# First feed-forward: the first two gate blocks from the scaled residual, with norm and shift joined in behind the products

## The chip, the cores and the metric

The kernel runs on one core of one Trainium2 chip. The metric is the device time of one execution in microseconds (us). Five engines work side by side, each through its own instructions in order: TensorE (PE, with its weight loads shown as PEld), VectorE (DVE), ScalarE (ACT), GpSimd (POOL) and the queue of transfers (SP).

## The reference

Two blocks of two layers each stand behind each other. The change touches the seam in layer 0 of the first block, between the state-space mixer and the feed-forward network. With x of 256 tokens by 1024 channels:

```
g   = gelu(y)
x   = x + gate1 * (g * sigmoid(g @ w_glu + b_glu))
h   = rms_norm(x, norm2_g) * (1 + scale2) + shift2
ff  = (silu(h @ w_gate) * (h @ w_up)) @ w_down
x   = x + gate2 * ff
```

`rms_norm` divides each token by the root of its mean square (plus 1e-6) and multiplies each channel by its gain. The feed-forward width is 2816, which is 22 blocks of 128 columns.

## The kernel before, in words

Everything is held with channels on the partitions: x is a tile of 128 x 8 x 256, eight blocks `k` of 128 channels by 256 tokens. Products are made in three parts, because weights and activations are each split into a rounded high part and the remainder: high by high, high by low, low by high (`mm3`). One such part is one matmul of 128 x 128 weights by 256 tokens. The weights come as tiles of 1 MB (`raw`, sixteen blocks of 128 x 128) through a ring of six buffers, in the order of one transfer queue (SP). Each tile is split in four quarters of 128 x 512: ACT makes the high part (`whi`), DVE the low part (`wlo`), and the four buffers of each are used in turn, so that a split waits until PE has finished the quarter four places back.

A scheduler orders each engine's instructions from the order in which the code was written; stretches under `manual_schedule` keep the written order on PE.

The stretch concerned:
- `proj(glu, ...)` multiplies by w_glu, two column blocks at a time (tiles `ps_mm`). `evac` then makes for each block `ob` the sigmoid (`sg`, ACT), its product with gelu (`sg`, DVE) and the new residual (`x`, DVE), and hands the square (`sq`, ACT) to `sumsq`. POOL adds the first six squares; the sum over channels is made by products with a matrix of ones into `ps_aux`.
- `root()` closes the sum, scales it (`rstd`, DVE) and takes the power -1/2 (`rstd`, POOL).
- `spread` copies it out along the free axis (`sprd`, ACT) and transposes it, so that every partition holds the factor of each token (L330).
- `ffn(0)` splits the first tile of gate weights ahead (`early`), then `normed` makes for each k the scaled x (`nrm`, DVE), adds the shift and rounds (`hh`, ACT) and makes the remainder (`hl`, DVE).
- For each p of 11, the products of two gate blocks (`pg`) and two up blocks (`pu`) follow, 48 matmuls each. For p = 0 and gate they go channel block by channel block, as `hh` and `hl` come. Then come silu (ACT), the product with `pu` (DVE) and its split (`ah`, `al`).
- After each of the 22 groups of 48 matmuls `pump` lets one step of a waiting matrix-vector product run (the modulations of the next layer): for the first six groups these are four operations `acc` of 128 x 512 on DVE each, from one tile `kvada`.

Of the kernel before, what the change touches and what calls it, by code (L numbers as in the profile page):

```python
# [9 lines left out]
F32 = mybir.dt.float32  # L10
F32R = mybir.dt.float32r
I32 = mybir.dt.int32
AF = mybir.ActivationFunctionType
ALU = mybir.AluOpType
AX = mybir.AxisListType

D, T, FF = 1024, 256, 2816
# [204 lines left out]
class _Flow:  # L222
# [12 lines left out]
    def add(self, rank, steps):  # L235
        self.strands.append([rank, self.t, (), steps])
        self.strands.sort(key=lambda s: s[0])
# [44 lines left out]
def _go(steps, n=1 << 30):  # L282

    for _ in range(n):
        if next(steps, steps) is steps:
            break


class K:
# [100 lines left out]
    def stream(self, src):  # L390

        raw, cur = {}, {}

        def get(n, ahead=False):
            t, u = n // 16, n // 4
            if u not in cur:
                if t not in raw:
                    raw.clear()
                    raw[t] = self.wtile(src[t])
                cur[u] = self.wsplit(raw[t], (u % 4) * WS, WS)  # L400
            if ahead:
                return
            for o in [o for o in cur if o < u]:
                del cur[o]
            hi, lo = cur[u]
            s = slice((n % 4) * 128, (n % 4 + 1) * 128)
            return hi[:, s], lo[:, s]

        return get
# [235 lines left out]
    def s5(self):  # L645
        nc, tc, a, c = self.nc, self.tc, self.a, self.c
        cp = self.cp
        V, G, S_ = nc.vector, nc.gpsimd, nc.scalar
        with ExitStack() as ctx:
            pool = lambda name, bufs=1: ctx.enter_context(tc.tile_pool(name=name, bufs=bufs))  # L650
            sm, big = pool("s5sm"), pool("s5big")
# [3 lines left out]
            B8 = lambda tag, shape, name, n=1, dt=F32: (old if tag in ("bc", "D", "P") else big).tile(  # L655
                shape, dt, tag=tag, name=name, bufs=n)
# [13 lines left out]
            box = []  # L670
# [15 lines left out]
            t = lambda n, w=32: sm.tile([128, w], F32, name="d_" + n)  # L686
# [25 lines left out]
            rs = sm.tile([128, 8], F32, name="rs")  # L712
# [91 lines left out]
            for e in range(8):  # L804
# [18 lines left out]
                for q in range(4):  # L823
                    o = psK[32 * q:32 * q + 32, 0:128]
# [18 lines left out]
            U = B8("U", [128, 16, 128], "U")  # L843
# [3 lines left out]
            for h in range(2):  # L847
                f = slice(8 * h, 8 * h + 8)
# [3 lines left out]
                for j4 in range(2):  # L852
# [4 lines left out]
                    o = U[:, 8 * h + 4 * j4:8 * h + 4 * j4 + 4].rearrange("p j n -> p (j n)")  # L857
# [38 lines left out]
            for k in range(1, 8):  # L896
                n = 4 if k < 7 else 3
                a8 = lambda k: A8[:, k].unsqueeze(1).to_broadcast([128, n, 2, 32])
                u2 = sm.tile([128, 4, 2, 32], F32, tag="u2", name="u2", bufs=2)
                f = slice(k, k + 8 * n - 7, 8)  # L900
# [4 lines left out]
            for b in range(1, 4):  # L905
# [6 lines left out]
                for e, q in ((0, QP[:, 0:1, 0:7].to_broadcast([128, 2, 7, 32])), (1, QP[:, 1:3, 0:7])):  # L912
                    o = (St[:, 8 * b, ::-1] if e else St[:, 8 * b]).unsqueeze(1).to_broadcast([128, 7, 2, 32])
                    self.mul(w1[:, e], o, q.rearrange("p r k g -> p k r g"))
                if b < 3:
                    o = St[:, 8 * b + 8]
                    self.add(o, o, v[:, 0])
                    self.add(o, o, v[:, 1])
                o = St[:, 8 * b + 1:8 * b + 8]
# [60 lines left out]
            x1 = x0  # L980

            add, root = self.sumsq()

            def evac(ob, ps):
                sg = self.np.tile([128, T], F32, tag="sg", name="sg")
                self.act(sg, ps, AF.Sigmoid, bias=self.col("bglu", ob))
                self.mul(sg, sg, gT[:, ob].rearrange("p t c -> p (t c)"))
                self.stt(x1[:, ob].rearrange("p (c t) -> p c t", t=8), sg.rearrange("p (t c) -> p c t", t=8),
                         self.mods[0][:, 16 + ob:17 + ob], x0[:, ob].rearrange("p (c t) -> p c t", t=8), ALU.mult, ALU.add)
                add(ob, x1[:, ob])  # L990

            self.proj(glu, 0, 8, list(range(8)), lambda k: gh[:, k], lambda k: gl[:, k], evac, 24, True, True)
            self.xr = root()
            self.x = x1

# [85 lines left out]
    def ffn(self, l):  # L1083
        nc, tc, x, m = self.nc, self.tc, self.x, self.mods[l]
        self.lo = [nc.vector]
        with ExitStack() as ctx:
            self.parts(ctx, 1)
            pool = ctx.enter_context(tc.tile_pool(name=f"ffn{l}", bufs=1))
            if l:
                self.deepen(3)  # L1090
                self.fill.append(self.last(pool))
            g = self.gain(m[:, 32:40], self.col("n2", 8 * l, 8), f"g2_{l}")
            gu = self.stream(self.a[f"gu{l}"])
            with self.early(gu):
                hi, lo = self.normed(x, self.spread(self.xr, 1), g, m[:, 24:32])
            self.after = self.lowed
            ah = pool.tile([128, 22, T], F32R, name="ah")
            al = pool.tile([128, 22, T], F32R, name="al")
            for p in range(11):
                if p == 4 and l == 0:  # L1100
                    self.mla_tables()
                if p == 6:
                    self.mem_norm(l)
                pg, pu = self.ps(), self.ps()
                for i, ps in enumerate((pg, pu)):
                    if p or i:
                        for e in range(2):
                            for k in range(8):
                                wh, wl = gu(32 * p + 16 * i + 8 * e + k)
                                self.mm3(ps[:, e * T:(e + 1) * T], wh, wl, hi[:, k], lo[:, k], k == 0, k == 7)  # L1110
                    else:

                        w = [gu(n) for n in range(16)]
                        for k in range(8):
                            for e in range(2):
                                self.mm3(ps[:, e * T:(e + 1) * T], *w[8 * e + k], hi[:, k], lo[:, k], k + e == 0, k + e == 8)
                    self.pump()
                self.after = None
                t = pool.tile([128, 2 * T], F32, tag="ff", name="ff", bufs=2)
                self.act(t, pg, AF.Silu)  # L1120
                self.mul(t, t, pu)
                f = lambda z: z[:, 2 * p:2 * p + 2].rearrange("p a t -> p (a t)")
                self.split(f(ah), f(al), t)

            if l == 0:
                self.table(AF.Sqrt)
            else:
                self.drain()
            add, root = self.sumsq()

            def evac(ob, ps):
                self.stt(x[:, ob], ps, m[:, 40 + ob:41 + ob], x[:, ob], ALU.mult, ALU.add)
                add(ob, x[:, ob])

            def down():
                self.proj(self.stream(self.a[f"dn{l}"]), 0, 22, list(range(8)), lambda k: ah[:, k], lambda k: al[:, k], evac, 12, single=True)
                self.drain()


            rest = iter(itertools.chain(self.mem_keys(l), self.mem_values(l)))  # L1140
            down()
            with tc.manual_schedule(engines={mybir.EngineType.PE}):
                self.lo = [nc.vector, nc.gpsimd]
                _go(rest, 2)
                r = root()
                _go(rest, 2)
                rs = self.spread(r, 1)
                _go(rest)
            self.lo = [nc.vector]
            if l:  # L1150
                self.wparts, self.npart = self.base, 0
                self.win = self.stream(self.a["win"])
                for n in range(3):
                    self.win(4 * n, True)
                self.h = self.normed(x, rs, self.col("pre", 0, 8))
            else:
                self.xn = self.memp.tile([128, 8, T], F32, name="xr")
                for k in range(8):
                    self.mul(self.xn[:, k], x[:, k], rs)
            self.shallow()  # L1160
            if not l:
                self.accc.close()
# [1092 lines left out]
```

## Time and profile before

| | |
|---|---|
| median of 3 runs | 1089.24 us (1083.6, 1089.24, 1095.2) |
| the profiled execution | 1079.3 us, span 1077.5 us |
| PE busy | 985.0 us, 91% |
| DVE busy | 809.5 us, 75% |
| ACT busy | 580.3 us, 54% |
| POOL busy | 268.9 us, 25% |
| chain that ended last | PE 65%, DVE 15%, issue 4%, ACT 3% |

Times in the trace are counted from the start of the span. The profiled execution is 9.9 us faster than the median of the three runs. Busy shares are means over many stages; what a stage waits for is read from its own rows. "PEclk" is the granted TensorE clock as a share of 2.4 GHz, so 0.50 is 1.2 GHz.

### The profile page before, as it was taken

The numbers are of one execution on the slowest core, as the hardware profiler recorded it, in microseconds if no ns is written. First come the engines' busy times: TensorE is split into PE (matmuls) and PEld (weight loads), VectorE is DVE, ScalarE is ACT, GpSimd is POOL, SyncE is SP. The second block draws the span as 40 slices with busy tenths as digits, with TensorE's granted clock in tenths as the row PEclk, the third lists the DMA queues.
The fourth block names the chain that finished last, engine by engine and source line by source line (L and its number), as shares of the span: only waits on it lengthen the run. The fifth ranks groups of instructions, "written<-read, shape, count | busy, mean of one in ns | idle before, by whom it ended". The sixth has DMA issues, their size and how long they took to land.

```text
span 1077.5 us, 21985 instructions
## 1 busy us (share of the span) xinstructions
PE 985.0 (91%) x8490; PEld 876.3 (81%) x8490; DVE 809.5 (75%) x1771; ACT 580.3 (54%) x1301; POOL 268.9 (25%) x300
## 2 busy tenths in 40 slices
PE   3988979999999988989999999988898899799996
PEld 1446968989999866889999999987887786699984
DVE  8846788989985788779756555688887735686995
ACT  6344555556544767646555544565444344575663
POOL 7960200030011551100000001453315132243430
PEclk9999989999999989999999999999999999999999
DMA  7999439877983241255755554241312142265321
GB/s 280 375 343 372 172 142 396 307 285 294 363 329 153 98 162 73 79 196 203 267 192 174 184 195 152 104 148 54 123 40 83 36 154 99 87 232 180 134 79 40
DMA packets 29416, 198.82 MB, mean 185 GB/s; under 512 B 3744, under 2 KB 3872, under 8 KB 6528
## 3 DMA queue, kind: packets, MB, share of 16 engines
q1 hardware_dynamic: 27936, 191.73, 48.2%
q10 hardware_dynamic: 720, 3.15, 0.8%
q0 software_dynamic: 656, 2.53, 0.7%
q8 instruction: 67, 1.10, 0.4%
q14 instruction: 37, 0.30, 0.1%
HBM read 195.30 MB, written 2.10 MB: 183 GB/s over the span
## 4 chain that ended last, share of the span: by engine, by line
PE 65%; DVE 15%; issue 4%; ACT 3%; POOL 2%; DMA 1%; POOLq 0%; DVEq 0%; ACTq 0%
PE ps_mm L327 50%; PE ps_aux L327 6%; DVE wlo L306 3%; PE ps_sv L327 3%; PE ps_el L327 2%; PE ps_aux L330 2%; PE ps_st L327 2%; ACT whi L376 1%; POOL sq L306 1%; DVE Upr L306 1%; DVE acc L323 1%; DMA raw<-in_gu 1%; DVE D L1738 1%; DVE shf L319 1%; DVE A L306 0%
## 5 line engine op out<-in xcount | busy, mean ns | idle before, releaser
L376 ACT CAST whi<-raw 128x512 fp32r<-128x512 f32 (+2 forms) x488 | 296.1, 613 | 271.5 <-PE ps_mm L327 230.0
L306 DVE TENSOR_TENSOR wlo<-raw,whi 128x512 fp32r<-128x512 f32 (+2 forms) x412 | 289.1, 714 | 128.4 <-ACT whi L376 127.7
L327 PE MATMUL ps_mm<-hh,whi 128*128 128x256 f32 x1064 | 306.8, 290 | 3.0 <-ACT hh L298 2.3
L327 PE MATMUL ps_mm<-hh,wlo 128*128 128x256 f32 x1064 | 300.6, 285 | 3.4 <-DVE wlo L306 3.3
L327 PE MATMUL ps_mm<-hl,whi 128*128 128x256 f32 x1064 | 300.0, 283 | 0.2
L327 PEld LDWEIGHTS ps_mm<-hh,whi 128*128 128x128 f32 x1064 | 202.0, 190 | 8.2 <-ACT hh L298 2.9
L327 PEld LDWEIGHTS ps_mm<-hh,wlo 128*128 128x128 f32 x1064 | 200.9, 190 | 8.8 <-DVE wlo L306 7.8
L327 PEld LDWEIGHTS ps_mm<-hl,whi 128*128 128x128 f32 x1064 | 201.9, 190 | 1.3 <-DVE hl L323 0.6
L306 POOL TENSOR_TENSOR wlo<-raw,whi 128x512 fp32r<-128x512 f32 (+2 forms) x76 | 100.3, 1321 | 244.1 <-ACT whi L376 218.5
L306 POOL TENSOR_TENSOR sq<-sq 128x256 f32<-128x256 f32 x20 | 23.4, 1171 | 415.0 <-ACT sq L298 264.7
L327 PE MATMUL ps_mm<-ah,whi 128*128 128x256 f32 x352 | 99.1, 282 | 0.0
L327 PE MATMUL ps_mm<-ah,wlo 128*128 128x256 f32 x352 | 99.0, 282 | 0.1
L327 PE MATMUL ps_mm<-al,whi 128*128 128x256 f32 x352 | 98.8, 281 | 0.0
L323 DVE SCALAR_TENSOR_TENSOR acc<-raw,cs,acc 128x512 f32<-128x512 f32 x112 | 80.0, 757 | 2.2 <-DMA raw<-in_kvada 2.1
L327 PEld LDWEIGHTS ps_mm<-ah,wlo 128*128 128x128 f32 x352 | 66.3, 189 | 2.8 <-issue 1.7
L327 PEld LDWEIGHTS ps_mm<-ah,whi 128*128 128x128 f32 x352 | 67.3, 191 | 0.9 <-ACT whi L376 0.8
L327 PEld LDWEIGHTS ps_mm<-al,whi 128*128 128x128 f32 x352 | 66.4, 189 | 0.0
L327 PE MATMUL ps_gv<-raw,crep 128*32 128x512 f32 x192 | 27.3, 624 | 17.0 <-DMA raw<-in_adaH 13.7
L327 PEld LDWEIGHTS ps_gv<-raw,crep 128*32 128x32 f32 x192 | 4.5, 110 | 22.0 <-DVE pwt L306 13.7
L327 PE MATMUL ps_mm<-gl,whi 128*128 128x256 f32 x64 | 18.9, 297 | 2.4 <-DVE gl L306 2.4
L327 PE MATMUL ps_mm<-whi,ch 128*128 128x512 f32 x48 | 19.5, 437 | 1.2 <-ACT ch L422 1.2
L306 POOL TENSOR_TENSOR CE<-CE,cem 128x512 f32<-128x512 f32 x16 | 20.5, 1321 | 0.0
(552 smaller groups left out, 2037.3 us busy)
## 6 DMA issues: line engine op xcount, KB each, us to landing
raw<-in_gu SPq DMA_DIRECT2D x44, 1024.0 KB, 5.1
raw<-in_ada SPq DMA_DIRECT2D x32, 1024.0 KB, 7.2
raw<-in_dn SPq DMA_DIRECT2D x22, 1024.0 KB, 5.0
raw<-in_win SPq DMA_DIRECT2D x15, 1024.0 KB, 4.9
raw<-in_adaH SPq DMA_DIRECT2D x8, 1024.0 KB, 6.4
raw<-in_kvada SPq DMA_DIRECT2D x8, 1024.0 KB, 6.5
raw<-in_ada1h SPq DMA_DIRECT2D x8, 1024.0 KB, 5.7
raw<-in_wout SPq DMA_DIRECT2D x8, 1024.0 KB, 4.9
```

What stands on the lines that cost most here:

```text
L306: return (eng or self.nc.vector).tensor_tensor(out=out, in0=a, in1=b, op=op)
L319: (eng or self.nc.vector).tensor_scalar(out=out, in0=a, scalar1=s1, scalar2=s2, op0=op0, **kw)
L323: return self.nc.vector.scalar_tensor_tensor(out=out, in0=a, scalar=s, in1=b, op0=op0, op1=op1, **kw)
L327: return self.nc.tensor.matmul(out, l, r, start=start, stop=stop, **kw)
L330: return self.nc.tensor.transpose(out, in_, self.ident)
L376: i = self.nc.scalar.copy(out=hi[:, :width], in_=raw[:, o:o + width])
L1738: V.tensor_reduce(out=D_[64 * h:64 * h + 64, 4 * i:4 * i + 4], in_=dm[:, :, h].rearrange("p c b i -> p c i b"), axis=AX.X, op=ALU.add)
```

## The change

The products of the first two gate blocks are taken from the residual times (gain times 1 + scale), `xgh` and `xgl`, which needs neither the token factor nor the shift. The token factor is multiplied in behind the products (`ff0`, DVE). The shift times the gate weights, one number per output column, is made by sixteen products with one moving column from the unsplit weight tile (`pb`, tile `ps_gv`) and enters as the bias of silu. The two up blocks and all later ones take `hh` and `hl` as before. The splits of the first gate tile now use the mixer's four pairs of buffers, and the order of the new products on PE is written out by hand.

```
@@ def stream
-        def get(n, ahead=False):
+        def get(n, ahead=False, keep=False):
...
-                    raw[t] = self.wtile(src[t])
+                    raw[t] = self.lastraw = self.wtile(src[t])
...
-            for o in [o for o in cur if o < u]:
+            for o in [o for o in cur if o < u and not keep]:
@@ def s5 (evac, and behind it)
                 add(ob, x1[:, ob])
+                if ob < 6:
+                    return
+                if ob == 6:
+                    box[:] = [self.gain(self.mods[0][:, 32:40], self.col("n2", 0, 8), "g2_0"),
+                              B8("C", [128, 8, T], "xgh", 4, F32R), B8("U", [128, 8, T], "xgl", 1, F32R)]
+
+                g, xh, xl = box
+                for k in range(7) if ob == 6 else (7,):
+                    self.act(xh[:, k], x1[:, k], AF.Identity, scale=g[:, k:k + 1])
+                    self.stt(xl[:, k], x1[:, k], g[:, k:k + 1], xh[:, k].bitcast(F32), ALU.mult, ALU.subtract)
 
             self.proj(glu, 0, 8, list(range(8)), lambda k: gh[:, k], lambda k: gl[:, k], evac, 24, True, True)
-            self.xr = root()
+            g, xh, xl = box
+            gu = self.stream(a["gu0"])
+            for n in range(4):
+                gu(4 * n, True)
+            with tc.manual_schedule(engines={mybir.EngineType.PE}):
+                pg, pb = self.ps(), self.ps("gv")
+                raw = self.lastraw
+                for k in range(8):
+                    if k == 6:
+                        self.xr = root()
+                    for e in range(2):
+                        self.mm3(pg[:, e * T:(e + 1) * T], *gu(8 * e + k, keep=True), xh[:, k], xl[:, k], k + e == 0, k + e == 8)
+                    if k == 6:
+
+                        for e in range(2):
+                            for j in range(8):
+                                self.mm(pb[:, e:e + 1], raw[:, 128 * (8 * e + j):128 * (8 * e + j) + 128],
+                                        self.mods[0][:, 24 + j:25 + j], j == 0, j == 7)
+                flat = sm.tile([128, 4, 8, 16], F32, tag="cem", name="sprd", bufs=2).rearrange("p a b e -> p (a b e)")
+                R = flat[:, 0:T]
+                S_.copy(out=R.rearrange("p (m d) -> p m d", m=2), in_=self.xr.unsqueeze(2).to_broadcast([128, 2, 128]))
+                rs = self.ps("aux")[:, :T]
+                for b in range(2):
+                    self.T(rs[:, 128 * b:128 * b + 128], R[:, 128 * b:128 * b + 128])
             self.x = x1
+            bias = self.cp.tile([128, 2], F32, name="gbias")
+            V.tensor_copy(out=bias, in_=pb[:, 0:2])
+            R = flat[:, T:]
+            S_.copy(out=R, in_=rs)
+            ff = self.cp.tile([128, 2 * T], F32, tag="gemv", name="ff0")
+            self.mul(ff.rearrange("p (e t) -> p e t", e=2), pg.rearrange("p (e t) -> p e t", e=2),
+                     R.unsqueeze(1).to_broadcast([128, 2, T]))
+            for e in range(2):
+                self.act(ff[:, e * T:(e + 1) * T], ff[:, e * T:(e + 1) * T], AF.Silu, bias=bias[:, e:e + 1])
+            self.begun = g, gu, rs, ff
@@ def ffn
-            with self.early(gu):
-                hi, lo = self.normed(x, self.spread(self.xr, 1), g, m[:, 24:32])
+            if l:
...
+            else:
+                g, gu, rs, ff = self.begun
+                for n in range(4):
+                    gu(16 + 4 * n, True)
+                hi, lo = self.normed(x, rs, g, m[:, 24:32])
...
+                    if done and not i:
+                        pass
+                    elif done:
+                        w = [gu(n) for n in range(16, 32)]
...
+                if done:
+                    self.mul(t, ff, pu)
```

How the order of instructions moves is shown at three places. On PE, behind the last product with w_glu, the kernel before goes from the sum of squares (`sq`) to the transposes of the token factor (`sprd`) and to the first gate products:

```order
L327 MATMUL ps_aux<-c_cst_75,sq 128x128 [waits Activation_49]
L327 MATMUL ps_aux<-c_cst_75,sq 128x128
L330 MATMUL ps_aux<-c_cst_75,sprd 128x128 [waits PE_49,Activation_49]
L330 MATMUL ps_aux<-c_cst_75,sprd 128x128
L327 MATMUL ps_mm<-hh,whi 128x256 [waits PE_49,Activation_49]
L327 MATMUL ps_mm<-hl,whi 128x256 [waits DVE_49]
```

In the changed kernel the same place on PE, from the last two sums of squares on, reads:

```order
L327 MATMUL ps_aux<-c_cst_75,sq 128x128 [waits Activation_49]
L327 MATMUL ps_aux<-c_cst_75,sq 128x128
L327 MATMUL ps_mm<-xgh,whi 128x256
...
L327 MATMUL ps_gv<-mods_82,raw 128x1 [waits DMAHW4_49]
L327 MATMUL ps_gv<-mods_82,raw 128x1 x15
L327 MATMUL ps_mm<-xgh,whi 128x256 [waits Activation_49]
...
L330 MATMUL ps_aux<-c_cst_75,sprd 128x128 [waits PE_49,Activation_49]
L330 MATMUL ps_aux<-c_cst_75,sprd 128x128
L327 MATMUL ps_mm<-hh,whi 128x256 [waits DVE_49,PE_49,Activation_49]
```

Between the sum of squares and the transposes now stand six products of k = 6, the sixteen products of the bias and six products of k = 7; the other 36 of the 48 stand ahead of the last sums.

On DVE the end of `evac` is shown, from the splits of the last w_glu quarter on; `x_108` is the residual, `xgl_1615` the new remainder, and `wlo_1676` to `wlo_1688` are the four quarters of the first gate tile, which before stood behind `rstd` as `wlo_1689` to `wlo_1701`. Before:

```order
L323 SCALAR_TENSOR_TENSOR x_108<-sg_1557,mods0_82,x_108 128x256 [waits DMASW2_49,DVE_49]
L323 SCALAR_TENSOR_TENSOR x_108<-sg_1564,mods0_82,x_108 128x256 [waits DVE_49]
L306 TENSOR_TENSOR sg_1606<-sg_1606,gT_1137 128x256 [waits DVE_49,Activation_49]
L323 SCALAR_TENSOR_TENSOR x_108<-sg_1606,mods0_82,x_108 128x256 [waits DVE_49]
L306 TENSOR_TENSOR sg_1645<-sg_1645,gT_1137 128x256 [waits Activation_49]
L323 SCALAR_TENSOR_TENSOR x_108<-sg_1645,mods0_82,x_108 128x256 [waits DVE_49]
L306 TENSOR_TENSOR gqk_2369<-c_cols_73 128x1 [waits PE_49]
L319 TENSOR_SCALAR rstd_1657<-ps_aux_1315 128x2 [waits PE_49]
L306 TENSOR_TENSOR wlo_1689<-raw_1686,whi_1688 128x512 [waits DMAHW4_49,Activation_49]
```

In the changed kernel:

```order
L306 TENSOR_TENSOR wlo_1676<-raw_1673,whi_1675 128x512 [waits DMAHW4_49,PE_49,Activation_49]
L323 SCALAR_TENSOR_TENSOR x_108<-sg_1557,mods0_82,x_108 128x256 [waits DMASW2_49,DVE_49]
L323 SCALAR_TENSOR_TENSOR x_108<-sg_1564,mods0_82,x_108 128x256 [waits DVE_49]
L306 TENSOR_TENSOR wlo_1680<-raw_1673,whi_1679 128x512 [waits PE_49,Activation_49]
L306 TENSOR_TENSOR wlo_1684<-raw_1673,whi_1683 128x512 [waits PE_49,Activation_49]
...
L323 SCALAR_TENSOR_TENSOR xgl_1615<-x_108,g2_0_1612,xgh_1614 128x256 [waits Activation_49]
L306 TENSOR_TENSOR wlo_1688<-raw_1673,whi_1687 128x512 [waits PE_49,Activation_49]
L306 TENSOR_TENSOR sg_1663<-sg_1663,gT_1137 128x256 [waits Activation_49]
L323 SCALAR_TENSOR_TENSOR xgl_1615<-x_108,g2_0_1612,xgh_1614 128x256 [waits DVE_49,Activation_49]
L323 SCALAR_TENSOR_TENSOR x_108<-sg_1663,mods0_82,x_108 128x256 [waits DVE_49]
```

Four splits and seven of the eight `xgl` now stand ahead of the last `x` on DVE; before, none of them did.

On ACT, from the token factor on, the kernel before reads:

```order
L1040 COPY sprd_1704<-rstd_1657 128x256 [waits Pool_49]
L298 ACTIVATE hh_1709<-nrm_1711,mods0_82 128x256 [waits DVE_49]
L298 ACTIVATE hh_1709<-nrm_1715,mods0_82 128x256 [waits DVE_49]
L298 ACTIVATE hh_1709<-nrm_1719,mods0_82 128x256 [waits DVE_49]
L298 ACTIVATE hh_1709<-nrm_1723,mods0_82 128x256 [waits DVE_49]
```

In the changed kernel:

```order
L1023 COPY sprd_1766<-rstd_1735 128x256 [waits Pool_49]
L1031 COPY sprd_1766<-ps_aux_1768 128x256 [waits PE_49]
L298 ACT_TABLE_LOAD
L298 ACTIVATE ff0_1775<-ff0_1775,gbias_1772 128x256 [waits DVE_49]
L298 ACTIVATE ff0_1775<-ff0_1775,gbias_1772 128x256
L298 ACTIVATE hh_1821<-nrm_1823,mods0_82 128x256 [waits DVE_49,Activation_49]
L298 ACTIVATE hh_1821<-nrm_1827,mods0_82 128x256 [waits DVE_49]
L376 CAST whi_1805<-raw_1803 128x512 [waits DMAHW5_49]
```

A copy, a table load and two silu now stand between the transposes and the first `hh`, and the splits of the first up tile behind the second `hh`.

## Rows read from the trace of the kernel before

**Rows 1.** Busy time of the engines in stretches around the seam: stretch (us), its length, then busy us (instructions) of PE, PEld, DVE, ACT and POOL, the granted clock, the share of the DMA engines and GB/s.
```profile
122.48:138.00 15.52, 13.58 (x109) 12.99 (x108) 14.25 (x24) 8.73 (x21) 6.35 (x5) 1.00 0.69 262
142.90:147.10 4.20, 4.20 (x18) 3.97 (x19) 3.83 (x10) 2.17 (x5) 0.00 (x0) 0.50 0.64 234
142.34:177.70 35.36, 32.85 (x237) 30.04 (x240) 34.74 (x61) 18.65 (x32) 0.00 (x0) 0.93 0.70 263
147.00:176.00 29.00, 27.05 (x215) 25.70 (x215) 28.94 (x49) 14.80 (x25) 0.00 (x0) 1.00 0.68 260
182.00:300.00 118.00, 116.05 (x958) 111.60 (x957) 109.62 (x199) 64.29 (x118) 8.42 (x6) 1.00 0.81 316
```

**Rows 2.** PE in order of time: start, duration, what, and in brackets the idle time before it and what ended that.
```profile
134.36 0.28 PE L327 MATMUL ps_mm<-gh,wlo 128*128 128x256 f32 x1
138.49 0.71 PE L327 MATMUL ps_aux<-c_cst,sq 128*128 128x128 f32 x4 [1.24 <-ACT sq L298]
141.10 0.69 PE L330 MATMUL ps_aux<-c_cst,sprd 128*128 128x128 f32 x2 [1.89 <-ACT sprd L1040]
142.90 0.58 PE L327 MATMUL ps_mm<-hh,whi 128*128 128x256 f32 x1 [1.12 <-ACT hh L298]
...
144.23 0.41 PE L327 MATMUL ps_mm<-hl,whi 128*128 128x256 f32 x1
144.44 0.41 PE L327 MATMUL ps_mm<-hh,wlo 128*128 128x256 f32 x1
...
147.31 0.28 PE L327 MATMUL ps_mm<-hl,whi 128*128 128x256 f32 x1
147.43 0.28 PE L327 MATMUL ps_mm<-hh,wlo 128*128 128x256 f32 x1
...
155.70 0.38 PE L327 MATMUL ps_mm<-hh,wlo 128*128 128x256 f32 x1 [0.90 <-DVE wlo L306]
...
170.27 0.39 PE L327 MATMUL ps_mm<-hh,wlo 128*128 128x256 f32 x1 [0.56 <-DVE wlo L306]
```

**Rows 3.** DVE in order of time, same columns.
```profile
125.00 1.30 DVE L306 TENSOR_TENSOR wlo<-raw,whi 128x512 fp32r<-128x512 f32 x2
129.10 2.98 DVE L306 TENSOR_TENSOR wlo<-raw,whi 128x512 fp32r<-128x512 f32 x3
137.34 0.65 DVE L323 SCALAR_TENSOR_TENSOR x<-sg,mods,x 128x256 f32<-128x256 f32 x1
139.24 0.16 DVE L319 TENSOR_SCALAR rstd<-ps_aux 128x2 f32<-128x2 f32 x1 [1.19 <-PE ps_aux L327]
142.88 0.89 DVE L323 SCALAR_TENSOR_TENSOR hl<-nrm,mods,hh 128x256 fp32r<-128x256 f32 x2 [0.18 <-ACT hh L298]
149.72 2.73 DVE L323 SCALAR_TENSOR_TENSOR acc<-raw,cs,acc 128x512 f32<-128x512 f32 x4
172.60 2.73 DVE L323 SCALAR_TENSOR_TENSOR acc<-raw,cs,acc 128x512 f32<-128x512 f32 x4
176.46 1.88 DVE L306 TENSOR_TENSOR wlo<-raw,whi 128x512 fp32r<-128x512 f32 x3
178.26 0.68 DVE L306 TENSOR_TENSOR al<-ff,ah 128x512 fp32r<-128x512 f32 x1
186.09 0.69 DVE L306 TENSOR_TENSOR ff<-ff,ps_mm 128x512 f32<-128x512 f32 x1 [0.55 <-PE ps_mm L327]
```

**Rows 4.** ACT in order of time, same columns.
```profile
121.97 0.84 ACT L298 ACTIVATE sg<-ps_mm,c_cols 128x256 f32<-128x256 f32 x2
138.03 0.42 ACT L298 ACTIVATE sq<-x 128x256 f32<-128x256 f32 x1 [1.17 <-DVE x L323]
140.64 0.40 ACT L1040 COPY sprd<-rstd 128x256 f32<-128x256 f32 x1
142.34 0.91 ACT L298 ACTIVATE hh<-nrm,mods 128x256 fp32r<-128x256 f32 x2 [1.29 <-DVE nrm L323]
153.03 1.28 ACT L298 ACT_TABLE_LOAD   x1
154.33 0.60 ACT L298 ACTIVATE ff<-ps_mm 128x512 f32<-128x512 f32 x1
```

**Rows 5.** POOL in order of time: two additions of squares, and the power of `rstd`.
```profile
129.16 2.37 POOL L306 TENSOR_TENSOR sq<-sq 128x256 f32<-128x256 f32 x2 [1.00 <-ACT sq L298]
139.48 1.13 POOL L306 TENSOR_TENSOR rstd<-rstd,eps 128x2 f32<-128x2 f32 x1 [3.89 <-DVE rstd L319]
```

**Rows 6.** Products of few columns elsewhere in the program: two of PE in order of time (four products of two columns with 128 x 128 weights, and four with weights of 64 columns; each product is two instructions), and the weight loads of such products with their shortest, median and longest duration in ns.
```profile
912.20 0.95 PE L327 MATMUL ps_st<-c_cst,gsq 128*128 128x2 f32 x8
907.08 0.66 PE L327 MATMUL ps_sv<-mpT,mv 128*64 128x128 f32 x8
L327 PEld LDWEIGHTS ps_st<-c_cst,gsq x24: 186/192/192, 807.5 to 912.9; 128*128 128x128 f32 x24
```

**Rows 7.** Transfers: the issue of the fourth feed-forward tile on the SP queue, and the page's line on this tensor's transfers (count, size, median us to landing).
```profile
141.85 0.33 SPq L357 DMA_DIRECT2D raw<-in_gu  x1
raw<-in_gu SPq DMA_DIRECT2D x44, 1024.0 KB, 5.1
```

More of the change, by code (lines that the diff above doesn't have):

```diff
@@ L1091, in ffn @@
                 self.fill.append(self.last(pool))
-            g = self.gain(m[:, 32:40], self.col("n2", 8 * l, 8), f"g2_{l}")
-            gu = self.stream(self.a[f"gu{l}"])
-            with self.early(gu):
-                hi, lo = self.normed(x, self.spread(self.xr, 1), g, m[:, 24:32])
+            if l:
+                g = self.gain(m[:, 32:40], self.col("n2", 8 * l, 8), f"g2_{l}")
+                gu = self.stream(self.a[f"gu{l}"])
+                with self.early(gu):
+                    hi, lo = self.normed(x, self.spread(self.xr, 1), g, m[:, 24:32])
+            else:
[3 more added lines that the diff above has]
+                hi, lo = self.normed(x, rs, g, m[:, 24:32])
             self.after = self.lowed
@@ L1103, in ffn @@
                     self.mem_norm(l)
-                pg, pu = self.ps(), self.ps()
+                done = p == 0 and l == 0
+                pg, pu = None if done else self.ps(), self.ps()
                 for i, ps in enumerate((pg, pu)):
-                    if p or i:
+                    if done and not i:
+                        pass
+                    elif done:
+                        w = [gu(n) for n in range(16, 32)]
+                        for k in range(8):
+                            for e in range(2):
+                                self.mm3(ps[:, e * T:(e + 1) * T], *w[8 * e + k], hi[:, k], lo[:, k], k + e == 0, k + e == 8)
+                    elif p or i:
                         for e in range(2):
@@ L1119, in ffn @@
                 t = pool.tile([128, 2 * T], F32, tag="ff", name="ff", bufs=2)
-                self.act(t, pg, AF.Silu)
-                self.mul(t, t, pu)
+                if done:
+                    self.mul(t, ff, pu)
+                else:
+                    self.act(t, pg, AF.Silu)
+                    self.mul(t, t, pu)
                 f = lambda z: z[:, 2 * p:2 * p + 2].rearrange("p a t -> p (a t)")
```

## The prediction

> **What bounds the kernel now.** I read the busy time by stretch first, then PE, DVE and ACT in order of time around the seam. The last product with w_glu starts on PE at 134.36 and the first gate product at 142.90 [rows 2]; between them PE has only the sums of squares and the two transposes. That hole of some 8.3 us is what the change fills. It is a chain: the last `x` on DVE (137.34, ready at 138.0 [rows 3]), its square on ACT (138.03 [rows 4]), the sums on PE (138.49 to 139.20 [rows 2]), `rstd` on DVE (139.24 [rows 3]) and on POOL (139.48, 1.13 us [rows 5]), the copy on ACT (140.64 [rows 4]), the transposes (141.10 [rows 2]), `nrm`, the first `hh` (142.34 [rows 4]). Behind the hole PE runs at a granted clock of 0.50, 1.2 GHz, until about 147.1 [rows 1]: starts 0.21 us apart, then 0.12 [rows 2].
>
> The second view matters more. From 147 to 176 DVE is busy 28.94 of 29.00 us, from the first `hh` to 177.7 it is 34.74 of 35.36, while PE still waits there for `wlo` (0.90 us before 155.70, 0.56 before 170.27) [rows 1, 2]. So for 35 us behind the hole DVE sets the pace, with the splits and the 24 `acc`; PE sets it only afterwards (116.05 of 118.00 us from 182 to 300 [rows 1]). An earlier gate product on PE buys nothing by itself; what counts is when DVE gets to `hh` and `hl`.
>
> **The change, part by part.** Times go against the profiled execution.
>
> *Moved products.* 48 products at 0.12 us, 5.7 us of PE, go into the hole. They save time only where PE sets the pace, so they stand under (e).
>
> *(a) DVE ahead of the last `x`.* By the order, seven `xgl` and four splits now stand ahead of it. An `xgl` is priced as an `hl`, two in 0.89 us, so 0.44; a split as one of the three in 1.88 us, so 0.63 [rows 3]. That is 7 x 0.44 + 4 x 0.63 = 5.6 us. DVE was busy 14.25 of 15.52 us in this stretch [rows 1], so 1.3 us are idle to take it: +4.3 us, the last `x` at 142.3. ACT has room (8.73 of 15.52 [rows 1]) for seven `xgh` and four casts. Lower end +2.1, if only half of it stands in the way; upper end +6, because beside POOL's additions (129.16 to 131.53 [rows 5]) three splits took 2.98 us where two took 1.30 [rows 3], 1.0 us more than by that pair, and a DVE without gaps meets more of them.
>
> *Square and sums* behind it take 1.2 us as before (138.0 to 139.20): 143.5. The 36 products queued ahead of the sums don't hold them up: 36 x 0.12 = 4.3 us from 134.6, with the fourth split done near 140.
>
> *(b) PE between sums and transposes.* Before, 1.9 us passed there (139.20 to 141.10), all of it the way over DVE, POOL and ACT. Now twelve gate products, 12 x 0.12 = 1.4 us, and the sixteen bias products stand in PE's queue ahead of the transposes. No row shows a product of one column; the nearest is two columns with 128 x 128 weights, eight instructions in 0.95 us with the last taking its own 0.25, so 0.10 each [rows 6]. Sixteen products are 32 instructions: 3.2 us. Together 4.6 us, hence +2.7. The way over POOL is hidden under it. Lower end 0.055 an instruction, from the weights of 64 columns (0.66 us for eight, last 0.28) [rows 6]: 1.8 us, +1.3. Upper end the weight load's own 0.19 us [rows 6]: 6.1 us, +5.6.
>
> *(c) From the transposes to the first `hh`.* Before, 1.24 us (141.10 to 142.34). Now ACT must first copy the factor (0.40), load the table of silu and make two silu of 256 columns; `hh` waits behind them in the same queue. Transposes 0.69, copy 0.40, load 1.30, two activations 0.84 (the two `sg`): 3.2 us [rows 2, 4], +2.0. `ff0` and `nrm` on DVE run under the load. The load is not new, but before it stood at 153.03, where ACT had time. After it the next activation starts 1.30 us behind the load's start (153.03, 154.33) [rows 4]. The Trainium skill, page "ScalarE: Activation LUTs", section "What ACT_TABLE_LOAD costs", gives such a switch a drain of about 1.38 us on top of the load, 2.66 us in all. By that (c) would be +3.4 and the forecast 1.4 us later; the row shows no drain, and the row decides.
>
> *(d) Edits at nothing.* `gbias` and `gqk` are small and DVE is idle there. The first tile's buffer is now held until the bias products have read it, so the fourth tile's load, issued at 141.85 before [rows 7], goes near 147; it lands some 5 us later and is split only behind the second and third tile's quarters, after 165. The next loads wait behind it on SP, with the same slack. The half clock stays: instead of the hole, PE now waits between the transposes and the first `hh` with its split weights, over 3 us, and the same stretch at 1.2 GHz follows.
>
> Sum so far: 4.3 + 2.7 + 2.0 = 9.0 us; the first `hh` at 151.3.
>
> *(e) What is given back.* From the first `hh` to 177.7 DVE does, in both orders, fourteen of the `nrm` and `hl`, 24 `acc`, the splits to the second quarter of the sixth tile, two `ff` and one `al`. It carries the 9.0 us to 186.7. Before, PE finished the third pair of blocks only at 186.09 (`ff` waits for PE [rows 3]), 8.4 us behind that point. With 48 products fewer PE can be nearer: two more splits and an `al` (1.9 us), then one quarter's twelve products (1.4 us) are the least, so at most 4.9 us come back, and nothing at least. I take 1.5, near the lower end: the last four `acc` now stand right ahead of those two splits, where before they were done (172.60 [rows 3]). From there PE sets the pace and the delay stays to the end.
>
> Net **+7.5 us**: 1079.3 to 1086.8. The median of the runs is 9.9 us above that execution, so I add to it: 1089.24 + 7.5, **1097 us**. That is 0.7%, inside the 1% that a measurement of this kernel can tell (its three runs span 1.1%).
>
> **The rivals.**
>
> *PE sets the pace (not slower).* If DVE's list behind `hh` were not the bound, the 48 products would count in full: 9.0 - 5.7 = +3.3; with (a) and (b) at their lower ends (2.2 and 1.4 less) -0.3: 1089 to 1092.5. For it: PE is busy 32.85 of the 35.36 us too [rows 1], so the two are close. Against it: DVE has 0.62 us free there and the work is the same. It decides itself at whether PE waits for `wlo` from 155 to 187. Chance 0.13.
>
> *The bias products at the price of their weight loads (slower by over 1%).* In PE's queue, between sums and transposes: 6.1 us instead of 3.2, nothing given back, (a) at its upper end: 7.5 + 2.9 + 1.5 + 1.7 = +13.6, 1103. For it: each of these products needs new weights, and they are unsplit. Against it: the row with 128 x 128 weights at 0.10 has these loads as well, though always the same matrix. From some 0.16 us an instruction on, with no give-back, it is over 1%. Chance 0.24.
>
> *The change does not fill the hole.* If a split or `xgl` comes so late that the 36 products end after 142.8, they push the sums behind them, us for us. By (a) they have over 1 us to spare. It would read as more of the second rival, and is in its chance.
>
> **How the numbers follow.** The forecast, +3.5 to +10.9, has 0.63. The range 1086 to 1106 takes in the forecast, most of the first rival and the second to its middle; I leave 0.1 out on each side, with the scatter of the runs. Slower by over 1%: the second rival's 0.24 less what scatter brings back, and the forecast's upper edge, 0.27. Faster by over 1% would need more than the whole hole and can only come from scatter: 0.03. Within 1%: 0.70.
>
> **What would show it.** In the changed trace: the last `x` some 4 us later; the sixteen bias products in 3 to 4 us; 7 us more until the transposes than before; table load and silu ahead of the first `hh`, that near 151; DVE without gaps for 35 us from there, PE waiting for `wlo`. Wrong would be: an `x` that is not late, bias products far from 0.10 us an instruction, or PE that does not wait for DVE behind `hh`.

## The result and the profile after

The changed kernel takes 1093.91 us in the median of 20 runs (1090.7 to 1101.0), the kernel before 1086.28 us (20 runs, 1079.85 to 1095.2). The ratio is 1.008, with a 95% interval of 1.0059 to 1.0102: **8.7 us slower** (6.4 to 11.1); the two medians stand 7.6 us apart. Forecast were +7.5 us and 1097 us, in a range of 1086 to 1106. The 1097 was counted from the median of three runs, 1089.24, which came out 3 us lower with twenty. Five of the changed kernel's runs, the profiled one among them, stand at 1098.8 to 1101.0 us, the other fifteen at 1090.7 to 1095.2.

The two profiled executions stand 21.6 us apart (1100.95 against 1079.3 us), far more than the medians. 8.9 us of that are one stall in the second block, which a second trace of the changed kernel doesn't have (last section). So I measure the change by distances inside a trace: from the first `x` of `evac` to the last `x`, to `rstd`, to the first `hh`, and to the issue of the tile `in_wdq` on SP, some 216 us behind the first `hh`, behind all of the first feed-forward. Both kernels were traced twice. Distances in us (the issue of `in_wdq` stands under "wdq"):

| trace | first x at | last x | rstd | first hh | wdq |
|---|---|---|---|---|---|
| before | 123.18 | 14.16 | 16.06 | 19.16 | 235.92 |
| before, again | 122.18 | 14.15 | 16.05 | 19.16 | 236.08 |
| after | 124.77 | 17.99 | 19.95 | 27.63 | 244.06 |
| after, again | 124.12 | 17.99 | 19.97 | 28.53 | 245.05 |

The change costs 8.1 us by the first traces and 9.0 by the second ones, and nearly all of it is there at the first `hh`: +8.5 and +9.4.

VectorE in the changed kernel, in order of time (start, duration, what, idle time before it and what ended that), which answers to [rows 3]:

```profile
127.19 0.48 DVE L323 SCALAR_TENSOR_TENSOR xgl<-x,g,xgh 128x256 fp32r<-128x256 f32 x1
...
132.76 1.85 DVE L323 SCALAR_TENSOR_TENSOR xgl<-x,g,xgh 128x256 fp32r<-128x256 f32 x2
...
142.76 0.68 DVE L323 SCALAR_TENSOR_TENSOR x<-sg,mods,x 128x256 f32<-128x256 f32 x1
144.32 0.48 DVE L323 SCALAR_TENSOR_TENSOR xgl<-x,g,xgh 128x256 fp32r<-128x256 f32 x1 [0.88 <-ACT xgh L298]
144.72 0.15 DVE L319 TENSOR_SCALAR rstd<-ps_aux 128x2 f32<-128x2 f32 x1
148.87 0.16 DVE L1029 COPY gbias<-ps_gv 128x2 f32<-128x2 f32 x1 [3.99 <-PE ps_gv L327]
149.68 0.16 DVE L306 TENSOR_TENSOR gqk<-c_cols 128x1 f32<-128x1 f32 x1 [0.66 <-PE ps_mm L327]
150.31 0.69 DVE L306 TENSOR_TENSOR ff<-ps_mm,sprd 128x512 f32<-128x512 f32 x1 [0.46 <-ACT sprd L1031]
151.09 0.87 DVE L323 SCALAR_TENSOR_TENSOR nrm<-x,g,ps_aux 128x256 f32<-128x256 f32 x2
```

Before, VectorE split the first gate tile behind `rstd`, in the hole:

```profile
139.32 2.50 DVE L306 TENSOR_TENSOR wlo<-raw,whi 128x512 fp32r<-128x512 f32 x4
```

Now it has done that ahead and stands idle there for 3.99 us, with the last `x` 3.8 us later.

PE in the changed kernel, same columns, which answers to [rows 2]:

```profile
143.20 1.46 PE L327 MATMUL ps_aux<-c_cst,sq 128*128 128x128 f32 x8
144.41 0.36 PE L327 MATMUL ps_mm<-xgh,whi 128*128 128x256 f32 x1
...
145.20 3.63 PE L327 MATMUL ps_gv<-mods,raw 128*128 128x1 f32 x32
148.69 0.36 PE L327 MATMUL ps_mm<-xgh,whi 128*128 128x256 f32 x1
...
149.49 0.38 PE L330 MATMUL ps_aux<-c_cst,sprd 128*128 128x128 f32 x2
153.85 0.58 PE L327 MATMUL ps_mm<-hh,whi 128*128 128x256 f32 x1 [3.99 <-DVE hl L323]
...
166.13 0.39 PE L327 MATMUL ps_mm<-hh,wlo 128*128 128x256 f32 x1 [2.53 <-DVE wlo L306]
```

The bias products take 145.20 to 148.69, 3.49 us. ScalarE, answering to [rows 4]:

```profile
149.90 0.37 ACT L1031 COPY sprd<-ps_aux 128x256 f32<-128x256 f32 x1 [3.78 <-PE ps_aux L330]
150.29 1.28 ACT L298 ACT_TABLE_LOAD   x1
151.59 0.91 ACT L298 ACTIVATE ff<-ff,gbias 128x256 f32<-128x256 f32 x2
152.40 0.89 ACT L298 ACTIVATE hh<-nrm,mods 128x256 fp32r<-128x256 f32 x2
```

And the busy time by stretch (length, then busy us and instructions of PE, PEld, DVE, ACT, POOL; clock, DMA share, GB/s), answering to [rows 1]:

```profile
152.40:187.76 35.36, 30.33 (x215) 29.33 (x216) 34.46 (x60) 18.09 (x34) 0.00 (x0) 0.84 0.68 255
153.85:160.00 6.15, 5.35 (x21) 4.76 (x22) 5.96 (x14) 3.23 (x7) 0.00 (x0) 0.50 0.29 97
```

Behind the first `hh` VectorE is busy 34.46 of 35.36 us, as before (34.74), and PE waits for `wlo`: 3.6 us between 152 and 198, where it was 1.9 in the same stretch before. Behind the first `hh` the half clock (0.50) now lasts 6.2 us instead of 4.2, and it comes back once more, as (d) below shows.

### The profile page after: what moved, and what is told of

It is laid out like the page before. It is cut to its first block, busy times and chain, and to the rows that moved or that the text cites. A ratio compares the mean times of both kernels' runs of the same rounds, so it can differ in the third digit from the quotient of the medians.

```text
span 1098.8 us, 22080 instructions
## 1 busy us (share of the span) xinstructions
PE 996.4 (91%) x8522; PEld 887.0 (81%) x8522; DVE 819.7 (75%) x1781; ACT 584.4 (53%) x1311; POOL 267.4 (24%) x300
## 3 DMA queue, kind: packets, MB, share of 16 engines
q0 software_dynamic: 656, 2.53, 0.7%
## 4 chain that ended last, share of the span: by engine, by line
PE 65%; DVE 16%; issue 4%; ACT 3%; POOL 1%; DVEq 0%; POOLq 0%; ACTq 0%
PE ps_mm L327 50%; PE ps_aux L327 6%; DVE wlo L306 4%; PE ps_sv L327 2%; PE ps_aux L330 2%; PE ps_el L327 2%; PE ps_st L327 2%; ACT whi L376 1%; DVE Upr L306 1%; DVE Us L1818 1%; DVE acc L323 1%; DVE D L1798 1%; DVE x L323 1%; DVE shf L319 0%; DVE hl L323 0%
## 5 line engine op out<-in xcount | busy, mean ns | idle before, releaser
L327 PEld LDWEIGHTS ps_gv<-raw,crep 128*32 128x32 f32 x192 | 4.4, 109 | 21.6 <-DVE pwt L306 13.6
L327 PE MATMUL ps_mm<-gh,wlo 128*128 128x256 f32 x64 | 19.0, 302 | 2.3 <-DVE wlo L306 2.3
```

Of the source, the lines that this page charges most:

```text
L327: return self.nc.tensor.matmul(out, l, r, start=start, stop=stop, **kw)
```

## The experiments

The theory: VectorE sets the pace behind the first `hh`, so the 48 products which PE has done ahead buy nothing, and the delay of the first `hh`, made of three parts, is carried whole. Each run's ratio to the kernel before is given with its interval; distances are those of the table, counted from the first `x`. Each order was traced once. The two traces of the changed kernel differ by 0.9 us at the first `hh` and by 1.0 at wdq, so a smaller difference between two orders counts only where rows show what made it.

**The bias products left out.**

```
@@ s5, for k == 6
-    for e in range(2):
-        for j in range(8):
-            self.mm(pb[:, e:e + 1], raw[...], self.mods[0][:, 24 + j:25 + j], j == 0, j == 7)
@@ silu of ff0: no bias
```

> The changed kernel without the sixteen bias products: the shift is left out of the first two gate blocks, and everything else keeps its order. The changed kernel stands 8.7 us above the kernel before. Theory (VectorE sets the pace behind the first hh, so the delay of the first hh is carried whole): the transposes start as soon as the copied factor is there, some 3.3 us sooner (the products took 3.5 us, from 145.20 to 148.69, and the factor was copied out at 146.1), and the time falls by 3 to 3.5 us, to about +5.3 us over the kernel before. Rival (what is won at the first hh is waited for again behind it): under 1 us.

Measured: first `hh` at 24.18 (3.5 sooner than in the first trace of after), wdq at 240.72 (3.3 sooner), ratio 1.0064 (1.0038 to 1.0089). ScalarE and SP of this kernel, whose first `x` is at 124.27:

```profile
148.45 0.89 ACT L298 ACTIVATE hh<-nrm,mods 128x256 fp32r<-128x256 f32 x2
364.99 0.33 SPq L357 DMA_DIRECT2D raw<-in_wdq  x1
```

What is won at the first `hh` is still there 216 us later: by the trace term (b) is shown, price and carry. The runs can't tell it, because the interval overlaps that of the changed kernel.

**Table load and silu late.**

```
@@ ffn, behind normed (and no longer in s5)
+    with tc.issue_after(self.rounded.ins):      # the last hh
+        for e in range(2):
+            self.act(ff[...], ff[...], AF.Silu, bias=bias[:, e:e + 1])
```

> The changed kernel with the table load and the two silu of ff0 behind the last hh on ScalarE, and so out of the way of the first hh. Theory: the first hh comes 2.1 us sooner (load 1.28, two silu 0.91, less the overlap with nrm), and the time falls by 1.5 to 2.1 us, to some +6.8 us over the kernel before. Rival (ScalarE's casts of the third weight tile, which now stand behind the table load, make VectorE's splits late): within 0.7 us of the changed kernel.

Measured: first `hh` at 27.07, only 0.56 sooner; wdq at 244.19, ratio 1.0077 (1.0054 to 1.0101). The theory missed; the rival's time came true, but not in its way. VectorE of this kernel, behind the transposes of 151.13:

```profile
152.10 0.69 DVE L306 TENSOR_TENSOR ff<-ps_mm,sprd 128x512 f32<-128x512 f32 x1 [0.61 <-ACT sprd L1031]
152.89 0.87 DVE L323 SCALAR_TENSOR_TENSOR nrm<-x,g,ps_aux 128x256 f32<-128x256 f32 x2
```

`nrm` stands behind `ff0`, which waits for the copy on ScalarE. That strand is nearly as long as load and silu. And the 0.56 are lost again by wdq. The scheduler now puts the casts of the first up tile behind the third `hh`, 29.3 us behind the first `x` instead of 28.4; that this is why was not tried.

**Four `acc` drawn into VectorE's idle time.**

```
@@ s5, behind root()
+    with tc.issue_after(self.closed.ins):      # rstd on VectorE
+        self.pump()
@@ ffn: the pump of p = 0, gate, left out in exchange
```

> The changed kernel with four of the acc operations (2.7 us of VectorE) drawn ahead from behind the last hl into the 4.0 us that VectorE stands idle between rstd and the bias copy; the hole and the first hh stay where they are. Theory (VectorE sets the pace for 35 us behind the first hh): the time falls by about 2.7 us, to +6 us over the kernel before. Rival (PE or the transfers set the pace there): no change, within 0.7 us of the changed kernel.

Measured: first `hh` at 28.19, the second `ff` 2.4 us sooner than in after (55.36 against 57.73), from the first `hh` to wdq 214.79 against 216.43 and 216.52 us. So 1.7 of the 2.7 us taken off VectorE's list behind `hh` come out as time, although PE's work there is the same. The first `hh` is 0.56 later than in the first trace of after, and not because of `acc`: they end at 147.46, and VectorE then still waits 1.34 us for the bias products. The clock fell ahead of the transposes here (last section). The ratio, 1.010 (1.0072 to 1.0128), doesn't show the gain: the runs scatter from 1091.7 to 1101.5.

**Bias products behind the transposes, and table load and silu late.**

```
@@ s5, PE's order
     self.T(rs[:, 128 * b:128 * b + 128], R[:, 128 * b:128 * b + 128])
+for e in range(2):
+    for j in range(8):
+        self.mm(pb[:, e:e + 1], raw[...], self.mods[0][:, 24 + j:25 + j], j == 0, j == 7)
@@ k == 6: without them; silu as in the kernel above
```

> The changed kernel with both put late: the sixteen bias products behind the transposes on PE, and the table load and the two silu behind the last hh on ScalarE. Theory (the two prices add up and are carried whole): 5 to 5.5 us less than the changed kernel, some +3.4 us over the kernel before; that is left of the first hh's 8.5 us what stands ahead of the last x on VectorE. Rival (the bias products, now beside the first hh, hold up the first up products by their 3.5 us): only 2 to 3 us less.

Measured: first `hh` at 23.64, wdq at 240.93 (3.1 sooner), ratio 1.0046 (1.0029 to 1.0063): 5.0 us slower than before, between theory and rival. The bias products took 4.6 us there (147.66 to 152.27), partly at half clock.

**All of `ff0` late.**

```
@@ ffn, behind normed
+    with tc.issue_after(self.rounded.ins): nc.scalar.copy(out=R, in_=rs)
+    with tc.issue_after(self.lowed.ins): self.mul(ff, pg, R)      # behind the last hl
```

> The kernel with both put late, and now also the copy of the factor and the product ff0 behind the last hl, so that nrm on VectorE follows the transposes at once. Theory (term (c) is not the table load alone but two strands of about equal length between the transposes and the first hh: load and silu on ScalarE, copy and ff0 ahead of nrm on VectorE; taking away one of them gives only its 0.6 us): the first hh comes 0.6 to 1.1 us sooner than with both put late, where it stood 23.6 us behind the first x, so at 22.6 to 23.0; the time is some 0.6 us less, about +4.4 us over the kernel before. Rival (copy, ff0, load and silu, now all later, hold up the first ah): no gain, or up to 1 us more.

Measured: first `hh` at 22.48, 1.2 sooner; wdq at 241.15, ratio 1.0048 (1.0016 to 1.008). The second strand of term (c) is shown at the first `hh`; behind it nothing is gained, and the rival's reason is in the trace: the first `ah` comes at 39.51, where it came at 38.75 with only load, silu and bias products late.

**Without `acc`, before and after.**

```
@@ gemv, for the tile kvada
-    self.stt(acc[:, f], w[:, f], c, acc[:, f], ALU.mult, ALU.add)
+    pass
```

> The kernel before with the 28 accumulating acc operations on the tile kvada left out (their result, the modulations modk, is wrong therefore; the transfers of the tiles stay). It is the base for the next kernel. 24 of them, some 16 us of VectorE, lie behind the first hh. Theory (VectorE sets the pace there): PE, which is idle 2.5 us of the 43.8 from the first hh (142.34) to the third ff (186.09), gets that back, and the four that are gone ahead of the mixer's products give up to 2 us more: 2 to 5 us faster than the kernel before. Rival (PE sets the pace): under 1 us behind the first hh.

> The changed kernel with the same 28 acc operations left out. Theory (with them VectorE sets the pace behind the first hh, so that the 48 products which PE has done ahead buy nothing; without them PE sets it, and they count): it stands only 3 to 5 us behind the kernel before without acc, against 8.7 us with acc (8.5 us at the first hh less some 4 to 5.7 us of PE). Rival (the delay of the first hh is carried whatever VectorE has to do): 8 to 9 us behind it, as with acc.

Measured, before: first `hh` 19.15, wdq 232.86, ratio 0.9979 (0.9955 to 1.0002); after: first `hh` 28.88, wdq 240.37, ratio 0.9986 (0.9963 to 1.0008). The runs tell neither from the kernel before. From the first `hh` to wdq it is 213.71 and 211.49 us, where it was 216.76 and 216.43 with `acc`. VectorE's list thus costs 3.1 us in the old order and 4.9 in the new one, and hides 1.9 us of what PE did ahead: the change gets back 2.2 us instead of 0.3. But not 4 to 5.7. PE's busy time in that stretch, summed over the view by stretch, does fall by 6.0 us (211.5 to 205.5), and its idle time rises by 3.8 (2.2 to 6.0): it comes to the up blocks sooner and waits for `hl` (2.1 us) and `wlo`. By the trace after stays 7.5 us behind, nearer the rival; 1.25 of them are the first `hh`, which is later than the 27.63 with `acc` because the clock fell earlier (last section). By the runs the two hardly differ (medians of 1083.39 and 1081.54 us). Which is right for the whole program stays open.

**Without `xgl`.**

```
@@ evac
-    self.stt(xl[:, k], x1[:, k], g[:, k:k + 1], xh[:, k].bitcast(F32), ALU.mult, ALU.subtract)
@@ products: xh[:, k] in the place of xl[:, k]
```

> The changed kernel without the eight xgl on VectorE: the low part of the scaled residual is left out, and the products with it take the high part once more, so that PE does as many products. Theory (xgl, 0.44 to 0.97 us each, and not the splits alone make the last x late): the last x comes 3 to 4.5 us sooner against the first one, all of it reaches the first hh, and the time falls by 3 to 4 us, to some +5 us over the kernel before. Rival (the four splits, which stay ahead of it, are what holds the last x up): it comes under 1.5 us sooner.

Measured: the last `x` at 15.62 (2.4 sooner), but `rstd` at 19.62 and the first `hh` at 28.85 (the clock fell during the bias products, which took 4.14 us); ratio 1.0094 (1.0066 to 1.0122). PE of this kernel:

```profile
137.38 0.39 PE L327 MATMUL ps_mm<-xgh,wlo 128*128 128x256 f32 x1 [0.64 <-DVE wlo L306]
...
141.19 1.06 PE L327 MATMUL ps_aux<-c_cst,sq 128*128 128x128 f32 x8
142.01 0.48 PE L327 MATMUL ps_mm<-xgh,whi 128*128 128x256 f32 x2
...
142.80 4.28 PE L327 MATMUL ps_gv<-mods,raw 128*128 128x1 f32 x32
146.94 0.77 PE L327 MATMUL ps_mm<-xgh,whi 128*128 128x256 f32 x2
```

The last `x` was ready at 138.97, yet the sums were issued at 141.19: they stood behind the 36 products, which had waited for a split until 137.38. Both theory and rival missed: there are two strands ahead of the sums.

**Without `xgl`, and the sums early on PE.**

```
@@ s5, PE's order (with all of ff0 late)
-    if k == 6: self.xr = root()
+    if k == 2: self.xr = root()
+    if k == 4:
+        for b in range(2):
+            self.T(rs[:, 128 * b:128 * b + 128], R[:, 128 * b:128 * b + 128])
```

> The kernel with all put late, without the eight xgl (the low part of the scaled residual is left out, its products take the high part once more), and on PE the sums of squares behind k = 1 instead of k = 5 and the transposes behind k = 3. Without xgl alone the last x came 2.4 us sooner, but the sums then stood behind the 36 products in PE's queue. Theory (VectorE's xgl and PE's queue are two strands of about equal length ahead of the sums, and term (a) is worth its 3 us only if both are taken away): rstd stands 17 to 17.5 us behind the first x instead of 20, the first hh 20 to 20.5, and the time is 2.5 to 3 us less than with all put late, +1.5 to +2 us over the kernel before. Rival (the four splits on VectorE still hold the sums up): rstd not before 19.

> The same order on PE (sums behind k = 1, transposes behind k = 3), with the eight xgl in place. Theory (with xgl it is VectorE that makes the last x late): rstd 20 us behind the first x as with all put late, and the time within 0.7 us of that kernel. Rival (PE's queue alone was the limit): rstd 2 us sooner, and 2 us less.

Measured without `xgl`: `rstd` at 17.53, as the theory said, wdq at 239.09 (2.1 sooner than with all late), but the first `hh` only at 22.35, and the ratio 1.0074 (1.0047 to 1.0101) doesn't follow. With `xgl`: `rstd` at 20.36, as the theory said, but first `hh` at 27.00 and wdq at 244.44, 3.3 us later than with all late instead of within 0.7; ratio 1.007 (1.0035 to 1.0105). Its trace is that of an execution of 1103.71 us, which has the stall of the last section. ScalarE, first without `xgl`, then with it:

```profile
145.78 0.91 ACT L298 ACTIVATE hh<-nrm,mods 128x256 fp32r<-128x256 f32 x2 [3.40 <-PE ps_mm L327]
...
153.86 0.91 ACT L298 ACTIVATE hh<-nrm,mods 128x256 fp32r<-128x256 f32 x2 [5.23 <-PE ps_mm L327]
```

The first `hh` waited for PE until the last of the 48 products ended: 3.40 us (145.45 + 0.28), and 5.23 us with `xgl` (153.54 + 0.28), where half of those products ran at half clock. `hh` needs nothing of that product's result; what it shares is probably its memory with the mixer's tiles, which I have not tried apart. In the changed kernel these products end ahead of the transposes, so this wait doesn't show.

**Both kernels once more.**

> The kernel before, once more, for its trace: in the changed kernel's trace the first x stands 1.6 us later than before, ahead of everything that the change adds. If that is scatter between executions, the first x here lies anywhere from 123 to 126.5 us; if it comes with the change (transfers in another order on SP), it stands at 123.2 again, within 0.3 us.

> The changed kernel once more, for its trace: from the first x to the first hh 27.6 us, and from the first hh to the issue of the tile wdq 216.4 us, each within 0.4 us, if these are the kernel's and not scatter. The first x at 124.8 within 0.3 us if its 1.6 us come with the change, anywhere from 122 to 126.5 if they are scatter.

Measured: before, the first `x` at 122.18, sooner than either reading allowed; after, at 124.12, and in the eight orders above with `acc` and the early products at 122.67 to 126.96. Ahead of it the engines have the same instructions, and it scatters by 4 us, but with the early products it is some 2 us later on the mean. That is left open. The distance from `hh` to wdq came out as expected (216.52), the one to the first `hh` 0.9 too long: the clock fell earlier (last section).

No version that does all of the work beats the kernel before; the nearest stand 5 us behind it.

## Why the prediction held, step by step

- **What bounds the kernel.** Right: 34.46 of 35.36 us of VectorE behind the first `hh`, and PE waiting for `wlo` there. Moving `acc` shows VectorE's pace (1.7 of 2.7 us), leaving it out shows PE 3 to 5 us behind it.
- **(a) VectorE ahead of the last `x`.** +4.3 forecast, +3.8 measured (17.99 against 14.16). Without `xgl` 2.4 of the 3.8 went; what the four splits make of the rest was not tried. The working was incomplete. PE was said to have over 1 us to spare; the products ended 0.7 us ahead of the last square (143.20; the square on ScalarE from 143.47, 0.42 long). The third rival, that the products push the sums, was that near, and it came true as soon as `xgl` was gone.
- **(b) PE between sums and transposes.** +2.7 forecast, +2.9 measured: from `rstd` to the transposes 4.77 instead of 1.86 us. 3.49 us for 32 instructions are 0.109 each, against 0.10 taken from the two-column products [rows 6]. The second rival, 0.19, fell.
- **(c) Transposes to the first `hh`.** +2.0 forecast, +1.7 measured (2.91 against 1.24). The size was right and the reason half: copy and `ff0` ahead of `nrm` are a second strand that the working put under the load. Load to next activation took 1.30 us again. The Trainium skill's page "ScalarE: Activation LUTs", section "What ACT_TABLE_LOAD costs", would have put some 1.4 us of drain on top; no row shows it, and the rows decide.
- **(d) Edits at nothing.** The fourth tile's load was issued at 148.86, forecast near 147. The half clock was not the same but 2 us longer, and it came back: PE's wait of 2.53 us before 166.13, with six `acc` ahead of the split on VectorE, was followed by some 3 us at 0.50, from 166.8 to 170.0. The kernel before ran at 1.00 there. VectorE of the changed kernel, and its busy time by stretch:

```profile
161.42 4.06 DVE L323 SCALAR_TENSOR_TENSOR acc<-raw,cs,acc 128x512 f32<-128x512 f32 x6
...
166.00:193.53 27.53, 27.16 (x202) 25.01 (x203) 25.34 (x42) 12.28 (x21) 0.00 (x0) 0.94 0.92 362
```

PE waited for `wlo` again at 176.91 (0.24 us), behind both stretches, so VectorE still set the pace. That the half clock cost nothing is argued from this and was not tried.
- **(e) Given back.** This term was mis-sized: 1.5 us forecast, 0.3 and 0.4 measured between the first `hh` and wdq. At the third `ff`, where the working ended, it is 2.6 (62.91 against 68.76, +5.85 instead of +8.47). But the delay does not stay as it is from there, as the prediction said: to wdq the changed kernel takes 175.30 us, the kernel before 173.01, with PE busy 2.3 us longer. Six products that it does only there make 0.7 us of that; the rest is open. The first traces show where the 48 products, 5.7 us of PE, went between the first `hh` and wdq. PE's busy time falls by only 2.9 us (212.27 to 209.42), since some 5.2 us more at half clock cost an estimated 2.6, half of them. Its idle time rises by 2.5 us (4.49 to 7.01).
- **Sum.** 3.8 + 0.1 + 2.9 + 1.7 = 8.5 at the first `hh` against 9.0, and 8.1 at wdq against 7.5. That the two lie so near is partly luck: (a) and (c) came out 0.8 us lower than forecast, and (e) gave back 1.2 us less. The first rival (PE sets the pace, +3.3) fell by the trace.

## What to carry to other kernels

Work moved into one engine's hole is worth only what the engine that sets the pace behind the hole is spared: count the moved instructions on that engine first. Where two strands of nearly equal length end at one wait, taking one away shows only the difference; take both before a term is called wrong. And where runs scatter as much as the effect, compare distances between two instructions of one trace.

## What the runs showed of the hardware

**A copy on VectorE that lasts as long as POOL's memsets.** VectorE in order of time, in the changed kernel's first trace:

```profile
703.20 7.70 DVE L1818 COPY Us<-c_cst 128x128 f32<-128x128 f32 x1
703.33 7.56 DVE L306 TENSOR_TENSOR hl<-nrm,hh 128x256 fp32r<-128x256 f32 x1
```

POOL in the same trace, the first and the last long memset of its row:

```profile
702.85 0.97 POOL L1700 MEMSET SAV<- 64x1024 f32 x1
...
709.83 0.97 POOL L1744 MEMSET BD<- 128x1024 f32 x1
```

And VectorE at the same place in its second trace:

```profile
703.66 1.18 DVE L1818 COPY Us<-c_cst 128x128 f32<-128x128 f32 x1
```

In both the copy starts 0.35 us behind the first long memset. Once it takes 1.18 us, once 7.70, and then it ends 0.1 us behind POOL's last memset (710.80). The long one is in five of the eleven traces with the early products and in none of the three without; those five executions took 1095.34 to 1103.71 us, the six others 1081.52 to 1093.11. From the issue of `in_wmv` to the next table load the changed kernel takes 66.55 us with the long copy and 57.65 without; a stretch at half clock behind it is part of that. This is the largest part of the difference between the two profiled executions. Why it comes and goes was not tried, so it stays open whether it comes more often with the change and so makes part of the 8.7 us.

**Slower VectorE operations beside POOL.** An `xgl` takes 0.48 us alone, and two take 1.85 beside POOL's additions of squares (131.03 to 134.33). Not all are slowed: three splits from 130.95 on, beside the same additions, took 1.89 us, where in the kernel before three took 2.98 [rows 3].

**The clock can fall while PE is busy.** The second trace of the changed kernel, by stretch, with the bias products from 144.56 to 148.06:

```profile
144.50:147.50 3.00, 3.00 (x30) 3.00 (x29) 0.00 (x0) 0.40 (x1) 0.55 (x1) 1.00 0.00 0
147.50:149.50 2.00, 2.00 (x14) 2.00 (x14) 0.16 (x1) 0.00 (x0) 0.00 (x0) 0.64 0.42 61
```

PE waits nowhere in this stretch, and still the granted clock goes from 1.00 to 0.50 within it, so that the six products behind start 0.21 us apart instead of 0.12. In the first trace it stayed at 1.00 until PE waited. That is the 0.9 us between the two traces at the first `hh`. Three more traces with the early products show such a fall with PE busy throughout: with `acc` in the hole from 149 on, without `acc` and without `xgl` from 146 on.
